# An MLP on one core: second product in one plain group and four groups of pairs, with half of its weights' sums made during the first product

## The chip, the core and the metric

The kernel runs on one core of a Trainium2 chip. The metric is the time of one execution on the device in microseconds (us); the median of three runs is compared.

The engines are named as the profile names them: PE multiplies matrices (PEld loads its weights), DVE, ACT and POOL work on vectors, and SP issues the transfers between the on-chip memory (SBUF, with PSUM for the products) and the DRAM. Each engine takes its instructions strictly in the order in which they stand in its queue. A matmul is given at 1.2 or 2.4 GHz; the profile's PEclk is the granted share of the higher one.

## What is computed

One layer of a decoder for 1032 columns of activations (1024 positions of a prompt and 8 sampled tokens), all in float32: an input projection, two groups of heads, an output projection, a norm, and the MLP that the change is about:

```python
x = layernorm(DN_ALPHA * x + mix, ln1_g, ln1_b)
h = jnp.square(jax.nn.relu(jnp.einsum('btd,df->btf', x, w_ff1)))   # 1024 -> 4096
x = layernorm(DN_ALPHA * x + jnp.einsum('btf,fd->btd', h, w_ff2), ln2_g, ln2_b)   # 4096 -> 1024
```

## The kernel before

Activations lie transposed: a tile is 128 features by 1032 columns, in two halves of 516 (`HN`), each in two pieces of 258 (`CH`). h has 32 such tiles. Every float32 operand X is split into hi (ACT rounds it, L111) and lo = X - hi (DVE or POOL, L112), and a product is hi.hi + hi.lo + lo.hi, so three matmuls; `split` and `product` (L1429 to L1440, matmul at L1438) are the helpers.

Most of the MLP runs by a scheme with seven products in place of eight (Strassen's, in Winograd's form). Weights are taken as 2x2 blocks A11, A12, A21, A22, the moving side as forms named B11, B21, B12, B22 and T1 to T4, where the T are sums of the B. The weights' sums are s1 = A21 + A22, s2 = s1 - A11, s4 = A12 - s2, s3 = A11 - A21. A unit makes its products in the order B21 (by A12), T1 (by s1), B11 (by A11), B22 (by s4), T2 (by s2), T3 (by s3), T4 (by A22).

**First product** (`ff1`, `pair`). The 32 tiles of h are made as 6 tiles without the scheme (`PLAIN`, in the stage before) and 13 pairs (`PAIRS`). A pair runs seven products of 24 matmuls, stores its four results B as tiles of `hd` in the DRAM, and for the pairs that the second product takes as pairs also the sums T1 to T4 in `ht`. `pair` loads two weight tiles `wpair`, makes s1 and s4 on DVE and s2 and s3 on POOL (L1464), evacuates PSUM with ACT and DVE, and stores.

**Second product** (`ff2`). It goes through `GROUPS` = [2, -3, -3, 2, -3, -3, 4]: a positive number is a plain group of so many tiles of h, a negative one a group of three pairs. A plain group (`plain_units`) has 16 units, one bank of PSUM each, added to `acc` by DVE (L1631, L1633). A group of pairs (`pair_units`, `pair_unit`) has four units q = 0 to 3 of seven products of 18 matmuls; a unit loads four blocks of weights into `w2raw` (six buffers), makes s1, s3, s4 on DVE and s2 on POOL (L1649), splits seven weights into `whi`/`wlo` or `wxh`/`wxl`, and adds seven times to `acc` (L1666).

What a group reads is loaded ahead, during the group before: a plain tile through `hraw` (two buffers), each of the 21 forms of a group of pairs through `hst` (four buffers, one row block of `hd` or `ht`), then split on ACT (t<-hst) and on DVE or POOL into one of 30 slots, which are used in turn (`RING`). After a plain group all 21 slots of the next group are free before it begins (`once`); after a group of pairs nine are (the forms B21, T1, B11, "early"), and the twelve others ("late") take slots that the last unit of the running group has still to read.

Within these loops the order on PE in the first product is as written; in the second product, and on the other engines everywhere, a scheduler with a simulated timeline sets the order of the queues at build time. SP has one queue: loads and stores of every kind stand in it one behind the other, each waiting for its buffer.

Of the kernel before, what the change touches and what calls it, by code (L numbers as in the profile page):

```python
# [9 lines left out]
F32 = mybir.dt.float32  # L10
F32R = mybir.dt.float32r
AF = mybir.ActivationFunctionType
OP = mybir.AluOpType
# [6 lines left out]
LBLK = [(0, 256), (768, 264), (256, 256), (512, 256)]  # L20
PBLK = [(0, 384), (384, 384), (768, 264)]
HN, CH = 516, 258
GROUPS = [2, -3, -3, 2, -3, -3, 4]
FIRST = [sum(abs(x) * (1 if x > 0 else 2) for x in GROUPS[:g]) for g in range(len(GROUPS))]
RING = "XXLLLLLLQBQBQBQBQBQBQBQQCQCQQB"
PLAIN = (0, 1, 14, 15, 28, 29)
PAIRS = [p for p in range(16) if 2 * p not in PLAIN]
FORMS = {"B11": "QL", "B21": "QL", "B12": "XX", "B22": "CL", "T1": "BQ", "T2": "BQ", "T3": "BQ", "T4": "BQ"}
TO = 2
TP = ((1, 3), (0, 1, 3), (0,), (2,))  # L30
LA = (384,384,384,256)
HE = {"B21": 0, "T1": 0, "B11": 0, "B22": 1, "T2": 1, "T3": 0, "T4": 1}
WE = (1, 0, 1, 0, 0, 0, 1, 1, 0, 1, 0)
# [26 lines left out]
class Kernel:  # L60
# [1305 lines left out]
    def out2(self, mixo, acc):  # L1366
        nc = self.nc
        V, G = nc.vector, nc.gpsimd
        self.fm = {}
        self.hd = self.dp.tile([32, 128, NT], F32, name="hd", tag="hd")  # L1370
        self.ht = self.dp.tile([14, 4, 128, HN], F32, name="ht", tag="ht")
        ws = self.resident(self.a["wout"][0], [self.x1slot("wr", w) for w in "LLLLLLBB"], self.tp)

        def units(c0):
            for n_ in range(8):
                ps = self.mmps(CH)
                yield from self.dense_q(ws[n_], mixo, c0, CH, ps)
                V.tensor_tensor(acc[n_][:, c0:c0 + CH], acc[n_][:, c0:c0 + CH], ps, op=OP.add)
                yield 3 * CH / 2400.0

        def norm(c, half, fill):
            put = (self.form("B11", c) + self.form("B21", c)) if not half else (self.form("B12", c) + self.form("B22", c))
            for wait in self.layer_norm_x1(acc, HN * half + CH * c, CH, put, LW[2 * c + half]):
                self.ahead(fill, wait)

        order = [(0, 0), (0, 1), (1, 0), (1, 1)]
        us = [units(HN * half + CH * c) for c, half in order]
        self.ahead(us[0], 99)
        chain = lambda *gs: (x for g in gs for x in g)
        norm(0, 0, chain(us[1], us[2]))  # L1390
        self.ahead(us[1], 99)
        norm(0, 1, chain(us[2], us[3]))
        self.ahead(us[2], 99)
        if TO == 0:
            self.t_forms(acc, 0)
        first = self.plain(0)
        norm(1, 0, chain(us[3], first))
        self.ahead(us[3], 99)
        if TO == 1:
            self.t_forms(acc, 0)  # L1400
        norm(1, 1, first)
        if TO == 2:
            self.t_forms(acc, 0)
        self.t_forms(acc, 1)
        self.ahead(first, 999)
        self.ahead(self.plain(1), 999)
# [46 lines left out]
    def pair(self, p):  # L1453
# [82 lines left out]
            out(f + 1, 0, P, m4)  # L1536
        yield

    def ff1(self):
        self.ps_ctx.close()  # L1540
        self.ps_ctx = ExitStack()
        self.sb = self.ps_ctx.enter_context(
            self.tc.tile_pool(name="sb", bufs=4, space=PSUM, reuse_waits="tile"))
        prev = iter(())
        for p in PAIRS:
            cur = self.pair(p)
            for i in range(5):
                next(cur)
                if i < 2:
                    next(prev, None)  # L1550
            prev = cur
        for _ in prev:
            pass
# [12 lines left out]
    def plain_forms(self, g, out):  # L1566
        nc = self.nc
        for j in range(GROUPS[g]):
            raw = self.h_load(FIRST[g] + j)
# [5 lines left out]
    def pair_forms(self, g, out):  # L1575
        n = -GROUPS[g]
        slots = {}
        once = GROUPS[g - 1] > 0
        early, late = ("B21", "T1", "B11"), ("B22", "T2", "T3", "T4")
# [39 lines left out]
    def plain_units(self, g, hs, acc):  # L1619
        V = self.nc.vector  # L1620
        nth = sum(1 for x in GROUPS[:g] if x > 0)
        for n_ in range(8):
# [13 lines left out]
    def pair_unit(self, g, q, fs, acc):  # L1636
        nc = self.nc
        V, G = nc.vector, nc.gpsimd
        E = lambda i: (V, G)[i]
        n = -128 * GROUPS[g]  # L1640
        A = {}
        for j in (1, 2, 3, 0):
            A[j] = self.tp.tile([128, 384], F32, name="w2raw", tag="w2raw", bufs=WB)[:, :n]
            nc.sync.dma_start(A[j], self.a["wff2_%d" % g][q][:, n * j:n * j + n])
        A11, A12, A21, A22 = (A[j] for j in range(4))

        def add(x, y, op, eng):
            z = self.wp.tile([128, 512], F32, name="wraw", tag="wraw", bufs=2)[:, :n]
            eng.tensor_tensor(z, x, y, op=op)  # L1649
            return z  # L1650
# [18 lines left out]
        product(Q, "B21", A12, E(WE[0]), True, True)  # L1669
        out(0, 0, Q)  # L1670
        yield
        s1 = add(A21, A22, OP.add, E(WE[1]))
        s2 = add(s1, A11, OP.subtract, E(WE[2]))
        T = self.bank()
        product(T, "T1", s1, E(WE[3]), True)
        out(1, 1, T)
# [2 lines left out]
        product(P, "B11", A11, E(WE[4]), True)  # L1679
        out(0, 0, P)  # L1680
        yield
        s4 = add(A12, s2, OP.subtract, E(WE[5]))
        product(T, "B22", s4, E(WE[6]), False, True)
        out(0, 1, T)
        yield
        product(P, "T2", s2, E(WE[7]), False)
        out(0, 1, P)
        yield
        s3 = add(A11, A21, OP.subtract, E(WE[8]))
        product(P, "T3", s3, E(WE[9]), False)  # L1690
        out(1, 1, P)
        yield
# [214 lines left out]
```

## Time and profile before

| | us |
|---|---|
| median of 3 runs | 1271.51 (1268.38 to 1274.57) |
| the profiled execution | 1271.54 |
| its span, first to last instruction | 1269.8 |
| PE busy in the span | 1210.6 (95%) |
| DVE, ACT, POOL busy | 833.7, 639.5, 509.0 |
| mean granted TensorE clock | 0.976 |

The profile is of one execution. Idle time of PE is what its row leaves open; a stretch at a granted clock of 1.00 without idle time runs at PE's pace. The first product lies at 629 to about 891 us from the span's start, the second from there to about 1208.

### The profile page before, as it was taken

The numbers are of one execution on the slowest core, as the hardware profiler recorded it, in microseconds if no ns is written. First come the engines' busy times: TensorE is split into PE (matmuls) and PEld (weight loads), VectorE is DVE, ScalarE is ACT, GpSimd is POOL, SyncE is SP. The second block draws the span as 40 slices with busy tenths as digits, with TensorE's granted clock in tenths as the row PEclk, the third lists the DMA queues.
The fourth block names the chain that finished last, engine by engine and source line by source line (L and its number), as shares of the span: only waits on it lengthen the run. The fifth ranks groups of instructions, "written<-read, shape, count | busy, mean of one in ns | idle before, by whom it ended". The sixth has DMA issues, their size and how long they took to land.

```text
span 1269.8 us, 25173 instructions
## 1 busy us (share of the span) xinstructions
PE 1210.6 (95%) x9268; PEld 1182.5 (93%) x9268; DVE 833.7 (66%) x1733; ACT 639.5 (50%) x1458; POOL 509.0 (40%) x540
## 2 busy tenths in 40 slices
PE   8999999889899899989999999999999999999996
PEld 7999999889899889989999999999989998989996
DVE  6477787778735885787743444444877768576667
ACT  5377676663656641267655555555545344242201
POOL 6243332362124651454533233332447542364214
PEclk9999999999989899899999999999989999989998
DMA  7322222132611261014435443444864535252202
GB/s 210 117 80 75 71 70 84 36 75 89 202 43 43 81 225 54 1 56 125 146 126 176 142 175 142 168 159 152 258 186 121 155 124 162 71 154 76 66 34 101
DMA packets 110075, 147.02 MB, mean 116 GB/s; under 512 B 30312, under 2 KB 65528, under 8 KB 109952
## 3 DMA queue, kind: packets, MB, share of 16 engines
q1 hardware_dynamic: 109952, 145.41, 36.6%
q8 instruction: 73, 1.20, 0.4%
q14 instruction: 50, 0.41, 0.1%
HBM read 100.31 MB, written 43.88 MB: 114 GB/s over the span
## 4 chain that ended last, share of the span: by engine, by line
PE 74%; DVE 12%; DMA 5%; issue 3%; ACT 3%; POOL 1%; SPq 1%; POOLq 0%; DVEq 0%; ACTq 0%
PE sb L1438 36%; PE mm L154 8%; PE mm L156 7%; PE mm L155 7%; DMA hst<-ht 2%; PE mm L1712 1%; PE mm L1714 1%; DVE wlo L112 1%; PE mm L1713 1%; DVE xB L1146 1%; DMA hst<-hd 1%; DVE acc L1132 1%; DMA hraw<-hd 1%; DVE uq L369 1%; DVE cx L303 1%
## 5 line engine op out<-in xcount | busy, mean ns | idle before, releaser
L112 POOL TENSOR_TENSOR wlo<-wraw,whi 128x512 fp32r<-128x512 f32 (+1 forms) x103 | 128.2, 1246 | 204.4 <-ACT whi L111 166.5
L111 ACT ACTIVATE whi<-wraw 128x512 fp32r<-128x512 f32 (+2 forms) x194 | 113.2, 585 | 169.8 <-PE sb L1438 105.9
L1438 PE MATMUL sb<-t,whi 128*128 128x258 f32 x1008 | 165.4, 287 | 6.4 <-ACT whi L111 4.8
L1438 PEld LDWEIGHTS sb<-t,whi 128*128 128x128 f32 x1008 | 141.4, 193 | 7.8 <-ACT whi L111 5.4
L1438 PE MATMUL sb<-xT,whi 128*128 128x258 f32 x832 | 133.8, 282 | 0.0
L154 PE MATMUL mm<-xhi,whi 128*128 128x344 f32 x384 | 126.3, 329 | 1.2 <-ACT zt L314 0.6
L155 PE MATMUL mm<-xlo,whi 128*128 128x344 f32 x384 | 123.9, 323 | 0.0
L156 PE MATMUL mm<-xhi,wlo 128*128 128x344 f32 x384 | 123.9, 323 | 0.0
L1438 PEld LDWEIGHTS sb<-xT,whi 128*128 128x128 f32 x832 | 114.0, 189 | 0.0
L1666 DVE TENSOR_TENSOR acc<-acc,sb 128x516 f32<-128x516 f32 x112 | 76.1, 686 | 56.5 <-PE sb L1438 56.4
L1438 PE MATMUL sb<-t,wlo 128*128 128x258 f32 x504 | 101.6, 286 | 3.0 <-DVE wlo L112 3.0
L1438 PE MATMUL sb<-xB,whi 128*128 128x258 f32 x624 | 100.2, 282 | 0.0
L112 DVE TENSOR_TENSOR wlo<-wraw,whi 128x512 fp32r<-128x512 f32 (+2 forms) x91 | 67.3, 743 | 42.5 <-ACT whi L111 42.5
L1438 PEld LDWEIGHTS sb<-xB,whi 128*128 128x128 f32 x624 | 85.7, 189 | 0.0
L1438 PE MATMUL sb<-xT,wlo 128*128 128x258 f32 x416 | 83.5, 282 | 0.0
L1438 PEld LDWEIGHTS sb<-t,wlo 128*128 128x128 f32 x504 | 79.0, 193 | 3.4 <-DVE wlo L112 3.4
L111 ACT ACTIVATE t<-hst 128x516 fp32r<-128x516 f32 x84 | 52.8, 634 | 51.0 <-DMA hst<-ht 23.9
L154 PEld LDWEIGHTS mm<-xhi,whi 128*128 128x128 f32 x384 | 72.4, 189 | 2.5 <-ACT sraw L295 1.1
L155 PEld LDWEIGHTS mm<-xlo,whi 128*128 128x128 f32 x384 | 72.4, 189 | 0.4 <-issue 0.4
L156 PEld LDWEIGHTS mm<-xhi,wlo 128*128 128x128 f32 x384 | 72.4, 188 | 0.4 <-issue 0.4
L112 POOL TENSOR_TENSOR t<-hst,t 128x516 fp32r<-128x516 f32 x36 | 52.3, 1459 | 35.4 <-ACT t L111 35.3
L1481 DVE TENSOR_TENSOR hst<-sb,hst 128x516 f32<-128x516 f32 x40 | 27.7, 694 | 58.9 <-PE sb L1438 58.9
(512 smaller groups left out, 3527.3 us busy)
## 6 DMA issues: line engine op xcount, KB each, us to landing
hd<-hst SPq DMA_DIRECT2D x52, 258.0 KB
wpair<-in_wff SPq DMA_DIRECT2D x26, 512.0 KB
ht<-hsum SPq DMA_DIRECT2D x48, 258.0 KB
hst<-ht SPq DMA_DIRECT2D x48, 258.0 KB
w2raw<-in_wff SPq DMA_DIRECT2D x64, 192.0 KB
wraw<-in_win SPq DMA_DIRECT2D x40, 256.0 KB
hst<-hd SPq DMA_DIRECT2D x36, 258.0 KB
wraw<-in_wff SPq DMA_DIRECT2D x24, 256.0 KB
```

The lines of the kernel that those rows point to most:

```text
L111: nc.scalar.activation(hi, src, AF.Copy)
L112: (lo_eng or nc.vector).tensor_tensor(lo, src, hi.bitcast(F32), op=OP.subtract)
L154: nc.tensor.matmul(ps, hi[:, k % 4, :], mh, start=(k == 0), stop=False)
L155: nc.tensor.matmul(ps, hi[:, k % 4, :], ml, start=False, stop=False)
L156: nc.tensor.matmul(ps, lo[:, k % 4, :], mh, start=False, stop=(k == last))
L303: nc.vector.scalar_tensor_tensor(out, raw[:, j:j + NP], cw[:, t, j:j + 1], out, op0=OP.mult, op1=OP.add)
L369: V.scalar_tensor_tensor(u[:, cc], ps[cc // 2][:, cc % 2], self.s2[:, hc:hc + 1], dt[:, cc, None, :].to_broadcast([128, 2, 128]), op0=OP.m ...
L1132: V.scalar_tensor_tensor(x, x, self.lnp[:, 0, i:i + 1], rb, op0=OP.mult, op1=OP.mult)
L1146: nc.vector.scalar_tensor_tensor(lo, x, b, hi.bitcast(F32), op0=OP.add, op1=OP.subtract)
L1438: self.nc.tensor.matmul(ps[:, 512 * c:512 * c + CH], a[:, k, :], forms[c][k][b], start=(start and k == 0 and a is hi and b == 0), stop=(st ...
L1481: V.tensor_tensor(h3, self.banks(ps), h3, op=OP.add)
L1666: V.tensor_tensor(a, a, self.banks(ps), op=OP.add)
```

## The change

`GROUPS` becomes [4, -3, -3, -3, -3, 4], and `PLAIN` the tiles 0 to 3, 28 and 29. So the two plain groups of two tiles become one of four at the start, and the four groups of pairs follow one another. The number of matmuls stays.

For seven of the 16 units of pairs (`STORED`: q = 0 and q = 3 of groups 1, 2, 3, and q = 0 of group 4) the four sums of weights are made earlier. After the pairs 0, 1, 2, 4, 6, 8, 10 of the first product (`BATCH`) `weight_load` loads the four blocks of one unit into two slots (`wq`) that are idle in that stage, and `weight_sums` makes the sums in place on DVE within the next pair and stores them in the DRAM (`wd`). `keep_in_program_order` ties these loads and sums to their written place. In the second product such a unit loads seven tiles (A12, s1, A11, s4, s2, s3, A22) into the same six `w2raw` buffers, where it loaded four and made the sums.

```diff
-GROUPS = [2, -3, -3, 2, -3, -3, 4]
+GROUPS = [4, -3, -3, -3, -3, 4]
-PLAIN = (0, 1, 14, 15, 28, 29)
+PLAIN = (0, 1, 2, 3, 28, 29)
+BATCH = (0, 1, 2, 4, 6, 8, 10)
+STORED = [(g, q) for g in range(1, 5) for q in (0, 3) if (g, q) != (4, 3)]
...
+    def weight_load(self, i):
+        g, q = STORED[i]
+        n = -128 * GROUPS[g]
+        z = []
+        for j in range(2):
+            t = self.x1slot("wq", "X").bitcast(F32)
+            self.tc.keep_in_program_order(
+                self.nc.sync.dma_start(t[:, :2 * n], self.a["wff2_%d" % g][q][:, 2 * n * j:2 * n * j + 2 * n]))
+            z += [t[:, 0:n], t[:, n:2 * n]]
+        return i, n, z
+
+    def weight_sums(self, i, n, z):
+        A11, A12, A21, A22 = z
+        for k, o, x, y, op in ((0, A22, A21, A22, OP.add), (2, A21, A11, A21, OP.subtract),
+                               (1, A11, A22, A11, OP.subtract), (3, A12, A12, A11, OP.subtract)):
+            self.tc.keep_in_program_order(self.nc.vector.tensor_tensor(o, x, y, op=op))
+            self.nc.sync.dma_start(self.wd[i, k][:, :n], o)
...
         prev = iter(())
-        for p in PAIRS:
+        batch = None
+        for n_, p in enumerate(PAIRS):
             cur = self.pair(p)
             for i in range(5):
                 next(cur)
                 if i < 2:
                     next(prev, None)
+                if i == 1 and batch:
+                    self.weight_sums(*batch)
+            batch = self.weight_load(BATCH.index(n_)) if n_ in BATCH else None
             prev = cur
...
-        for j in (1, 2, 3, 0):
+        stored = STORED.index((g, q)) if (g, q) in STORED else None
+        for j in (1, 4, 0, 7, 5, 6, 3) if stored is not None else (1, 2, 3, 0):
             A[j] = self.tp.tile([128, 384], F32, name="w2raw", tag="w2raw", bufs=WB)[:, :n]
-            nc.sync.dma_start(A[j], self.a["wff2_%d" % g][q][:, n * j:n * j + n])
...
+            nc.sync.dma_start(A[j], self.a["wff2_%d" % g][q][:, n * j:n * j + n] if j < 4 else
+                              self.wd[stored, j - 4][:, :n])
...
+        def add(k, x, y, op, eng):
+            if stored is not None:
+                return A[3 + k]
```

Three places show how the queues move. DVE, in the first product, where one pair follows the other. Before:

```order
L1489 TENSOR_TENSOR hsum<-hst,hsum 128x516
L1464 TENSOR_TENSOR wraw<-wpair 128x512
L1481 TENSOR_TENSOR hst<-sb,hst 128x516
L112 TENSOR_TENSOR wlo<-wpair,whi 128x512
L112 TENSOR_TENSOR wlo<-wraw,whi 128x512
L1481 TENSOR_TENSOR hst<-sb,hst 128x516
```

After:

```order
L1492 TENSOR_TENSOR hsum<-hst,hsum 128x516
L1557 TENSOR_TENSOR wq<-wq 128x384
L1467 TENSOR_TENSOR wraw<-wpair 128x512
L1484 TENSOR_TENSOR hst<-sb,hst 128x516
L1557 TENSOR_TENSOR wq<-wq 128x384
L114 TENSOR_TENSOR wlo<-wpair,whi 128x512
L1557 TENSOR_TENSOR wq<-wq 128x384 x2
L114 TENSOR_TENSOR wlo<-wraw,whi 128x512
```

Of the four new sums two stand ahead of the low part of the pair's first weight, and two ahead of that of its second.

SP, at the end of the first product (in_wff_0 holds the weights of the first plain group, in_wff_1 and wd those of the first group of pairs). Before:

```order
L1558 DMA hraw<-hd 128x1032
L1484 DMA hd<-hst 128x516
L1558 DMA hraw<-hd 128x1032
L1644 DMA w2raw<-in_wff_1 128x384 x2
L1609 DMA wraw<-in_wff_0 128x256
L1644 DMA w2raw<-in_wff_1 128x384 x4
```

After:

```order
L1487 DMA hd<-hst 128x516
L1583 DMA hraw<-hd 128x1032 x2
L1670 DMA w2raw<-in_wff_1 128x384
L1634 DMA wraw<-in_wff_0 128x512
L1670 DMA w2raw<-wd 128x384
L1670 DMA w2raw<-in_wff_1 128x384
L1670 DMA w2raw<-wd 128x384 x3
L1634 DMA wraw<-in_wff_0 128x512
L1614 DMA hst<-hd 128x516
L1583 DMA hraw<-hd 128x1032
L1487 DMA hd<-hst 128x516
```

The first tile of h now stands behind a store, and the third, which the plain group of four also needs at its start, behind the weights.

ACT, where one group of pairs follows another: w2raw_12479 and wraw_12542 are the first and second weight of unit q = 0 of the new group (for B21 and T1), the t are its late forms. Before, from group 1 to group 2:

```order
L111 ACTIVATE t_12233<-hst_12231 128x516
L111 ACTIVATE whi_12488<-w2raw_12479 128x384
L111 ACTIVATE t_12263<-hst_12261 128x516
L111 ACTIVATE t_12291<-hst_12289 128x516
L111 ACTIVATE whi_12547<-wraw_12542 128x384
L111 ACTIVATE h_12538<-hraw_12536 128x1032
```

After, from group 2 to group 3 (w2raw_13587 and w2raw_13589 are those two weights, the second of them a stored s1; wxh_13625 is a weight of the unit before):

```order
L113 ACTIVATE t_13307<-hst_13305 128x516
L113 ACTIVATE wxh_13625<-w2raw_13412 128x384
L113 ACTIVATE t_13336<-hst_13334 128x516
L113 ACTIVATE whi_13602<-w2raw_13587 128x384
L113 ACTIVATE t_13341<-hst_13339 128x516
L113 ACTIVATE t_13371<-hst_13369 128x516
L113 ACTIVATE whi_13659<-w2raw_13589 128x384
```

The weight for T1 comes from a load in place of a sum, and stands behind the same two forms as before.

## Rows read from the trace of the kernel before

**Rows 1.** The page: the chain that ended last, by engine.

```profile
PE 74%; DVE 12%; DMA 5%; issue 3%; ACT 3%; POOL 1%; SPq 1%; POOLq 0%; DVEq 0%; ACTq 0%
```

**Rows 2.** By stretch: length; PE, PEld, DVE, ACT, POOL busy (count); PEclk, DMA share, GB/s.

```profile
629.00:888.00 259.00, 259.00 (x2159) 259.00 (x2158) 110.27 (x164) 139.92 (x233) 84.43 (x65) 1.00 0.44 154
888.00:912.00 24.00, 24.00 (x202) 24.00 (x201) 18.33 (x29) 13.59 (x25) 8.74 (x6) 1.00 0.86 276
912.00:933.00 21.00, 17.25 (x114) 16.41 (x114) 17.20 (x24) 11.58 (x21) 15.65 (x12) 0.84 0.72 209
...
977.00:995.00 18.00, 15.21 (x122) 14.60 (x122) 16.14 (x17) 9.95 (x18) 16.94 (x12) 1.00 0.63 196
...
1046.00:1075.00 29.00, 26.74 (x213) 25.71 (x213) 23.74 (x39) 12.89 (x27) 8.30 (x7) 1.00 0.54 161
...
1129.00:1143.00 14.00, 11.03 (x68) 10.60 (x67) 9.95 (x11) 6.58 (x11) 8.47 (x7) 0.76 0.57 172
1143.00:1160.00 17.00, 15.63 (x126) 15.10 (x125) 12.49 (x15) 5.28 (x11) 9.29 (x7) 1.00 0.32 94
...
1202.00:1209.00 7.00, 5.43 (x44) 5.01 (x43) 1.67 (x3) 0.00 (x0) 0.00 (x0) 1.00 0.00 0
```

**Rows 3.** PE's queue in order of time: start, length, [idle before, releaser].

```profile
925.40 1.23 PE L1438 MATMUL sb<-t,whi 128*128 128x258 f32 x4 [2.80 <-ACT whi L111]
...
979.85 0.39 PE L1438 MATMUL sb<-t,whi 128*128 128x258 f32 x1 [0.93 <-ACT whi L111]
981.73 0.51 PE L1438 MATMUL sb<-t,wlo 128*128 128x258 f32 x2 [1.14 <-DVE wlo L112]
990.91 0.76 PE L1438 MATMUL sb<-t,whi 128*128 128x258 f32 x4 [0.72 <-DVE acc L1666]
```

**Rows 4.** ACT's queue ahead of the wait at 979.85.

```profile
976.50 0.64 ACT L111 ACTIVATE t<-hst 128x516 fp32r<-128x516 f32 x1 [1.61 <-DMA hst<-hd]
977.05 0.51 ACT L111 ACTIVATE whi<-w2raw 128x384 fp32r<-128x384 f32 x1
978.04 1.34 ACT L111 ACTIVATE t<-hst 128x516 fp32r<-128x516 f32 x2 [0.48 <-DMA hst<-ht]
979.29 0.51 ACT L111 ACTIVATE whi<-wraw 128x384 fp32r<-128x384 f32 x1
```

**Rows 5.** SP's queue: the loads of those forms.

```profile
974.80 1.48 SPq L1589 DMA_DIRECT2D hst<-ht  x3
```

**Rows 6.** DVE and POOL at the same place.

```profile
980.03 1.65 DVE L112 TENSOR_TENSOR wlo<-wraw,whi 128x384 fp32r<-128x384 f32 x1
...
985.74 0.55 DVE L1649 TENSOR_TENSOR wraw<-w2raw,wraw 128x384 f32<-128x384 f32 x1
...
979.45 1.81 POOL L112 TENSOR_TENSOR t<-hst,t 128x516 fp32r<-128x516 f32 x1
```

**Rows 7.** Form splits on ACT (tile t) while the first plain group runs.

```profile
895.00:926.00 31.00, 7.49 (x57) 7.20 (x58) 10.37 (x12) 12.71 (x20) 11.46 (x8) 0.98 0.81 243
```

**Rows 8.** Groups of instructions, 888 to 1209: the sums of weights, and the adds.

```profile
L1649 DVE TENSOR_TENSOR wraw<-w2raw 128x384 f32<-128x384 f32 x32 | 32.7, 1040 | 2.5 <-POOL wlo L112 1.5 <-POOL wxl L112 0.8
L1649 POOL TENSOR_TENSOR wraw<-wraw,w2raw 128x384 f32<-128x384 f32 x16 | 18.1, 1132 | 18.3 <-DVE wlo L112 11.7 <-PE sb L1438 4.3 <-DMA w2raw<-in_wff 1.8
L1633 DVE TENSOR_TENSOR acc<-acc,sb 128x516 f32<-128x516 f32 x16 | 10.6, 684 | 1.2 <-PE sb L1438 1.2
```

**Rows 9.** First product: DVE ahead of a pair's first weight, and PE's use of it.

```profile
719.28 0.68 DVE L112 TENSOR_TENSOR wlo<-wpair,whi 128x512 fp32r<-128x512 f32 x1
...
721.36 0.64 PE L1438 MATMUL sb<-xT,whi 128*128 128x258 f32 x4
721.84 0.40 PE L1438 MATMUL sb<-xT,wlo 128*128 128x258 f32 x2
```

**Rows 10.** Tiles of h at the end of the first product: SP's load, ACT's split.

```profile
882.49 0.42 SPq L1558 DMA_DIRECT2D hraw<-hd  x1
...
888.32 1.07 ACT L111 ACTIVATE h<-hraw 128x1032 fp32r<-128x1032 f32 x1 [0.34 <-DMA hraw<-hd]
```

More of the change, by code (lines that the diff above doesn't have):

```diff
@@ L1370, in out2 @@
         self.hd = self.dp.tile([32, 128, NT], F32, name="hd", tag="hd")
+        self.wd = self.dp.tile([len(STORED), 4, 128, 384], F32, name="wd", tag="wd")
         self.ht = self.dp.tile([14, 4, 128, HN], F32, name="ht", tag="ht")
@@ L1641, in pair_unit @@
         A = {}
-        for j in (1, 2, 3, 0):
+        stored = STORED.index((g, q)) if (g, q) in STORED else None
+        for j in (1, 4, 0, 7, 5, 6, 3) if stored is not None else (1, 2, 3, 0):
             A[j] = self.tp.tile([128, 384], F32, name="w2raw", tag="w2raw", bufs=WB)[:, :n]
-            nc.sync.dma_start(A[j], self.a["wff2_%d" % g][q][:, n * j:n * j + n])
-        A11, A12, A21, A22 = (A[j] for j in range(4))
-        def add(x, y, op, eng):
+            nc.sync.dma_start(A[j], self.a["wff2_%d" % g][q][:, n * j:n * j + n] if j < 4 else
+                              self.wd[stored, j - 4][:, :n])
+        A11, A12, A21, A22 = (A.get(j) for j in range(4))
+        def add(k, x, y, op, eng):
+            if stored is not None:
+                return A[3 + k]
             z = self.wp.tile([128, 512], F32, name="wraw", tag="wraw", bufs=2)[:, :n]
@@ L1671, in pair_unit @@
         yield
-        s1 = add(A21, A22, OP.add, E(WE[1]))
-        s2 = add(s1, A11, OP.subtract, E(WE[2]))
+        s1 = add(1, A21, A22, OP.add, E(WE[1]))
+        s2 = add(2, s1, A11, OP.subtract, E(WE[2]))
         T = self.bank()
@@ L1681, in pair_unit @@
         yield
-        s4 = add(A12, s2, OP.subtract, E(WE[5]))
+        s4 = add(4, A12, s2, OP.subtract, E(WE[5]))
         product(T, "B22", s4, E(WE[6]), False, True)
@@ L1688, in pair_unit @@
         yield
-        s3 = add(A11, A21, OP.subtract, E(WE[8]))
+        s3 = add(3, A11, A21, OP.subtract, E(WE[8]))
         product(P, "T3", s3, E(WE[9]), False)
```

## Prediction

> **What bounds the kernel now.** I read the chain that ended last first: PE holds 74% of it [rows 1], so time is gained only where PE stops or runs at its lower clock. The table by stretch says where in the MLP that is [rows 2]. In the first product PE is busy for 259.00 of 259.00 us at a clock of 1.00: nothing is to be gained there, and the change can only cost. The second product loses time in patches. Idle time is length less PE's busy time: 3.75 us at 912 to 933, where the first plain group hands over to the first group of pairs; 2.79 at 977 to 995, between two groups of pairs; 2.26 at 1046 to 1075, around the second plain group; 2.97 and 1.37 at 1129 to 1160, again between two groups of pairs; 1.57 at 1202 to 1209, at the end. That is 14.7 us. Twice PE stops long enough for the clock to fall to the lower of its two levels for a while: 21 us at 0.84 and 14 us at 0.76 are 3.4 us each. So 21.5 us are lost in all; the four stretches of the second product that are not shown run full. If the change took all of it, the profiled execution of 1271.5 us (its span is 1269.8; the median of the runs, 1271.51, is the same number) would take 1250: the floor.
>
> Then I read what ends the waits. At 925.40 and 979.85 it is ACT's high part of a weight, at 981.73 DVE's low part, at 990.91 DVE's add to acc [rows 3]. ACT was not busy before 979.85: its queue holds two forms ahead of that weight, which waited for their loads [rows 4], and those loads were issued one by one, as buffers of hst came free [rows 5]. The low part then took 1.65 us on DVE, where a sum of the same size takes 0.55, while POOL ran a form's low part from 979.45 to 981.26 [rows 6]. So a switch between groups of pairs is a queue of late forms through four buffers, in which a weight that PE needs stands behind.
>
> **The start of the second product (cost).** The plain group of four needs four tiles of h, of which hraw holds two. A tile's load took from 882.49 to 888.32, 5.8 us [rows 10]. In the new order of SP the first two leave together after a store, at about 882.5, and land by 889; their splits end near 890.3 and 892.6, and PE, which ends the first product at about 891.4, starts with them on four banks. The third tile's load can leave when the first's low part is done, 890.3, and lands at 896; PE has used up the first two tiles after 48 matmuls, at 0.12 us each (four start in 0.48 us) [rows 9], 5.8 us, at 897.2. Third and fourth tile then come within a microsecond of need. I put 1.0 us here, between 0 and 3.
>
> **From the plain group to the first group of pairs (gain).** Before, 21 forms have the time of 16 units of 12 matmuls, 23 us; ACT made 20 form splits in 31 us [rows 7], so the forms are late, and the stretch loses 3.75 + 3.4 = 7.2 us [rows 2]. Now the units have 24 matmuls, 46 us, in which that pace gives 30. I leave 0.3 us, between 0 and 3.75. Of DVE's adds to acc 16 of 0.68 us go as well [rows 8], 11 us of an engine that is idle for more; alone they are worth nothing, as are the eight weight splits that become wider. The second plain group's 2.26 us go with that group, but in its place stands a switch between two groups of pairs.
>
> **The three switches between groups of pairs.** There were two, at 2.79 and, with its clock and the stretch behind it, 2.97 + 3.4 + 1.37 = 7.7 us [rows 2]. Removed near each are the sums of two units (one unit at the last): per unit three on DVE, 2 x 1.04 + 0.56 = 2.6 us, and one on POOL, 1.13 us [rows 8], that also blocked POOL's queue while it waited for DVE. Seven units: 18 us of DVE and 8 of POOL, nearly all beside PE's work, so their sum is no gain; what counts is the order on ACT. There the weight for T1 stands behind the same two late forms as before; it no longer waits for a sum, but it was not the sum that held it. For group 1 to 2 slots and order are as before; DVE's add that ended late at 990.91 stood behind work that goes. I take 2.0, between 0 and 7.7.
>
> The switches from 2 to 3 and 3 to 4 are new in kind: the late forms take slots in another order, and three of them can be split only when the old group's last unit has done its third product (B11), where before six had gone by then. From there I count on ACT: two waiting forms 1.28, the low part that frees a buffer 0.70, the next load about 2.7 (the third load of rows 5 was issued at about 976.0, and its split, the second of the two at 978.04, began at 978.7 [rows 4]), then four forms at 0.64 and three weights at 0.51 [rows 4], the last of them T1's: 8.8 us. PE has 58 matmuls in that time, T4 of the unit before, B22, T2 and four of the new B21: 7.0 us. It is 1.8 us late, and the low parts behind it on DVE and POOL add some 1.2, as at 981.73 [rows 3]: 3.0 us each. Nothing in the trace shows such a switch; if the reading fails it costs nothing, or, with the form queue late as at the first group as well, 7.2 more. I take 3.0, nearest to the 2.79 of rows 2.
>
> **The sums in the first product (cost).** 28 sums of 0.55 us alone [rows 6], 2.2 us in seven pairs of 20 us, of which DVE is busy 43% [rows 2]. Two stand ahead of the low part of a pair's first weight. That low part ended at 719.96, PE used it at 721.84 [rows 9]: 1.1 us fit into 1.9. The 14 loads and 28 stores, 11 MB more at 154 GB/s, stand on SP among stores that nobody waits for and ahead of weight loads for which wpair has the buffers of two pairs. I put 0 here. The cover is that 1.9 us.
>
> **The sum.** 1.0 + 0.3 + 2.0 + 3.0 + 3.0 + 1.6 at the end (unchanged, and not shortened: that unit is not stored) = 10.9 us lost, where 21.5 were. 1271.5 - 10.6 = **1261 us**.
>
> **The rivals.**
> *The first product pays.* DVE took 1.65 us for what takes 0.55 alone, with POOL at work [rows 6]. Were both sums ahead of the low part held up by a POOL instruction of 1.3 us, they would take 3.7 us, 1.8 more than the margin, in seven pairs: 12.6 us, **1273.5**. Against it: POOL is busy for a third of that stretch [rows 2]. The Trainium skill, SBUF — State Buffer, section "Who interferes with whom", says that a DVE instruction with two inputs in SBUF contends with a GpSimd instruction that reads SBUF, and that the one that starts later is blocked for the whole of the other; by that rule each of the 28 new sums could wait so, and rows 6 agree.
> *The clock falls at both new switches.* 3.4 us each [rows 2] on top of 3.0: **1268**. [...]
> *The sums were not it, and switches stay as they were*, three at the mean of 2.8 and 7.7: 15.8 + 2.9 lost, **1269**.
> *Switches without waits*, since ACT, DVE and POOL run ahead once the sums are gone: at most 1 us each, **1256**, in good runs 1253.
> *Slower: the forms starve.* A stored unit issues seven weight loads in place of four, on the queue in which the forms' loads stand, and into six buffers, so SP waits in front of a weight while a form's buffer is free. If at every switch the forms come as late as they did at the first group, 7.2 us with the clock on top of 3.0, the three cost 30.6 and the whole 33.5: 1271.5 + 12.0 = **1283.5**. It decides from 8.3 us per switch (25 for the three, to lose 27.9). For it: forms already came by load, not by slot [rows 4]. Against: the DMA share there is 0.32 to 0.63, and was 0.86 and 0.72 where the forms were late [rows 2].
>
> **How the numbers follow.** Forecast, 1256 to 1266: 0.50. No waits at the switches: 0.12. Clock at the new switches: 0.15. Sums were not it: 0.05. First product pays: 0.08. Forms starve: 0.10. A measurement of this kernel tells some 0.5% from no change, 1265.2 to 1277.9. Faster than that: 0.12 and all but the upper edge of the forecast, 0.60. Slower: 0.10. Within: 0.30. For 8 times in 10 the range runs from 1253 to 1275; it leaves out the starving forms and the ends of the others.
>
> **What would show it.** In the profile after: the first product at 1.00 and without idle time (if not, the first product pays); a full stretch where plain tiles give way to the first pairs, and no low clock there; three switches some 60 us apart, each with a wait for ACT's high part of T1's weight behind forms, longer at the second and third. Wrong would be the prediction if ACT's waits for forms at the switches were gone, or if PE waited there for forms (t) themselves and not for weights.

## The result, and the profile after

The changed kernel takes 1263.73 us (median of six runs, 1262.25 to 1266.08) where the kernel before took 1271.25 beside it: a ratio of 0.9943, interval 0.9925 to 0.9961. The forecast was 1261 and faster, range 1253 to 1275. The profiled execution took 1262.84 us, its span is 1260.7.

First the stretches of the changed kernel that the argument needs, with the columns of [rows 2]: length; PE, PEld, DVE, ACT, POOL busy (count); PEclk, DMA share, GB/s.

```profile
629.00:888.00 259.00, 259.00 (x2159) 259.00 (x2158) 123.14 (x192) 138.29 (x232) 84.33 (x65) 1.00 0.57 196
...
893.00:908.00 15.00, 13.50 (x108) 12.87 (x107) 8.43 (x11) 9.01 (x15) 5.11 (x3) 1.00 0.99 335
908.00:990.00 82.00, 82.00 (x685) 82.00 (x684) 52.79 (x77) 32.98 (x60) 33.53 (x27) 1.00 0.50 151
990.00:1012.00 22.00, 19.81 (x161) 19.20 (x160) 13.17 (x20) 12.00 (x23) 14.45 (x12) 1.00 0.82 258
...
1060.00:1090.00 30.00, 26.75 (x215) 25.88 (x214) 21.73 (x32) 12.85 (x26) 13.60 (x12) 1.00 0.68 206
...
1120.00:1128.00 8.00, 7.41 (x61) 7.20 (x61) 4.79 (x6) 5.53 (x10) 8.00 (x7) 1.00 0.69 213
...
1140.00:1150.00 10.00, 7.75 (x65) 7.54 (x64) 9.11 (x12) 3.42 (x6) 6.41 (x4) 1.00 0.38 112
...
1188.00:1200.00 12.00, 11.21 (x93) 11.00 (x92) 3.66 (x6) 0.00 (x0) 0.16 (x1) 1.00 0.14 45
```

The clock is 1.00 in every stretch; both falls of [rows 2] are gone in this execution. (Its mean clock over the whole span is 0.982; the five other executions list 0.976 to 0.979. So the clock was lower somewhere in them; where, no profile shows.) Length less PE's busy time is 1.50 us at the start, 0 from the plain group into the first pairs, 2.19, 3.25 and 0.59 + 2.25 at the three switches between groups of pairs, 0.79 at the end; with 0.08 at 1128 to 1140, not shown, 10.65 us in all. Before it was 14.7 us, and 6.8 more were lost by the low clock.

Then PE's waits of more than 0.25 us in the second product, in order of time, as in [rows 3]:

```profile
899.74 1.78 PE L1441 MATMUL sb<-h,whi 128*128 128x258 f32 x10 [0.59 <-ACT h L113]
905.04 0.51 PE L1441 MATMUL sb<-h,whi 128*128 128x258 f32 x2 [0.88 <-POOL h L114]
1000.55 0.75 PE L1441 MATMUL sb<-t,whi 128*128 128x258 f32 x4 [1.98 <-ACT whi L113]
1063.29 0.75 PE L1441 MATMUL sb<-t,whi 128*128 128x258 f32 x4 [1.12 <-ACT whi L113]
1073.28 0.75 PE L1441 MATMUL sb<-t,whi 128*128 128x258 f32 x4 [1.43 <-DVE acc L1695]
1083.23 0.51 PE L1441 MATMUL sb<-t,wxl 128*128 128x258 f32 x2 [0.54 <-DVE wxl L114]
1127.79 0.75 PE L1441 MATMUL sb<-t,whi 128*128 128x258 f32 x4 [0.59 <-ACT whi L113]
1147.95 0.51 PE L1441 MATMUL sb<-t,wxl 128*128 128x258 f32 x2 [2.25 <-DVE wxl L114]
1196.90 0.75 PE L1441 MATMUL sb<-t,wxh 128*128 128x258 f32 x4 [0.79 <-DVE acc L1695]
```

Each of the three switches begins with a wait for ACT's high part of a weight (1.98, 1.12, 0.59). The waits at 1073, 1083 and 1147 are for DVE, and no step of the prediction put them there.

The first switch is the one foretold. ACT, POOL and SP there:

```profile
997.33 0.63 ACT L113 ACTIVATE t<-hst 128x516 fp32r<-128x516 f32 x1 [1.78 <-DMA hst<-ht]
999.45 0.63 ACT L113 ACTIVATE t<-hst 128x516 fp32r<-128x516 f32 x1 [1.48 <-DMA hst<-ht]
999.99 0.51 ACT L113 ACTIVATE whi<-w2raw 128x384 fp32r<-128x384 f32 x1
...
992.62 3.04 POOL L114 TENSOR_TENSOR t<-hst,t 128x516 fp32r<-128x516 f32 x2 [0.33 <-ACT t L113]
...
994.50 0.32 SPq L1614 DMA_DIRECT2D hst<-ht  x1
994.88 0.43 SPq L1670 DMA_DIRECT2D w2raw<-wd  x1
995.41 0.85 SPq L1614 DMA_DIRECT2D hst<-ht  x2
```

The weight for T1 stands on ACT behind a form, split at 999.45, that waited for its load. That load is the first of the two at 995.41. Its buffer had come free at 993.93, with the first of POOL's two low parts; but on SP it stood behind the load of 994.50, which waited for a buffer until DVE's low part ended at 994.48, and behind a weight's. From its issue to the form's split it took 4.0 us, where the load of 994.50 took 2.8 to the split at 997.33.

The last big wait has another origin. DVE and POOL ahead of 1147.95:

```profile
1142.63 2.93 DVE L114 TENSOR_TENSOR wr<-hst,wr 128x512 fp32r<-128x512 f32 x1
1145.48 1.35 DVE L114 TENSOR_TENSOR wlo<-w2raw,whi 128x384 fp32r<-128x384 f32 x1
1146.75 0.68 DVE L1695 TENSOR_TENSOR acc<-acc,sb 128x516 f32<-128x516 f32 x1
1147.35 0.55 DVE L114 TENSOR_TENSOR wxl<-wraw,wxh 128x384 fp32r<-128x384 f32 x1
...
1142.26 2.75 POOL L114 TENSOR_TENSOR h<-hraw,h 128x1032 fp32r<-128x1032 f32 x1
1144.95 1.46 POOL L1678 TENSOR_TENSOR wraw<-wraw,w2raw 128x384 f32<-128x384 f32 x1
```

The preparation of the last plain group is at work here: the low part of one of its weights (wr) takes 2.93 us on DVE, where the six of its kind that ran beside no POOL instruction took 0.68 to 0.69, and it ends 0.55 us after POOL is done with a tile of h. The next low part takes 1.35 for 0.55, beside POOL's sum. The low part that PE needs (wxl) stands behind both and behind an add.

### The profile page after: what moved, and what is told of

The parts are those of the page before. It is cut to its first block, busy times and chain, and to the rows that moved or that the text cites. A ratio compares the mean times of both kernels' runs of the same rounds, so it can differ in the third digit from the quotient of the medians.

```text
span 1260.7 us, 25210 instructions
## 1 busy us (share of the span) xinstructions
PE 1205.4 (96%) x9268; PEld 1177.4 (93%) x9268; DVE 811.1 (64%) x1716; ACT 637.3 (51%) x1450; POOL 497.4 (39%) x533
## 4 chain that ended last, share of the span: by engine, by line
PE 74%; DVE 13%; DMA 5%; ACT 3%; issue 3%; POOL 2%; SPq 0%; POOLq 0%; DVEq 0%; ACTq 0%
PE sb L1441 37%; PE mm L156 7%; PE mm L158 7%; PE mm L157 7%; DMA hst<-ht 1%; PE mm L1741 1%; DMA xraw<-in_xT 1%; DVE xB L1148 1%; DMA hst<-hd 1%; PE mm L1742 1%; PE mm L1743 1%; DVE acc L1134 1%; DVE wlo L114 1%; DMA hraw<-hd 1%; DVE cx L305 1%
## 5 line engine op out<-in xcount | busy, mean ns | idle before, releaser
L114 POOL TENSOR_TENSOR wlo<-wraw,whi 128x512 fp32r<-128x512 f32 (+1 forms) x88 | 109.1, 1241 | 188.6 <-ACT whi L113 167.9
L113 ACT ACTIVATE whi<-wraw 128x512 fp32r<-128x512 f32 (+1 forms) x164 | 100.3, 611 | 146.6 <-PE sb L1441 83.6
L1441 PE MATMUL sb<-t,whi 128*128 128x258 f32 x1008 | 162.5, 284 | 5.5 <-ACT whi L113 3.7
L1441 PEld LDWEIGHTS sb<-t,whi 128*128 128x128 f32 x1008 | 138.6, 190 | 6.7 <-ACT whi L113 4.3
L114 DVE TENSOR_TENSOR wlo<-wraw,whi 128x512 fp32r<-128x512 f32 (+1 forms) x76 | 57.1, 752 | 27.4 <-ACT whi L113 26.9
```

What stands on the lines that cost most here:

```text
L113: nc.scalar.activation(hi, src, AF.Copy)
L114: (lo_eng or nc.vector).tensor_tensor(lo, src, hi.bitcast(F32), op=OP.subtract)
L1441: self.nc.tensor.matmul(ps[:, 512 * c:512 * c + CH], a[:, k, :], forms[c][k][b], start=(start and k == 0 and a is hi and b == 0), stop=(st ...
```

## The experiments

The second column is the median with its ratio to the kernel before, the third PE's idle time from 893 to 1200 us of the profiled execution, the fourth the granted clock there. Waits at the very end of the second product lie behind 1200 us in the slower executions: 1.57 us for the kernel before, 0.78 each for the new grouping alone and the stored sums alone. "Unread" sums are made and stored in the first product but not used in the second.

| kernel | us, ratio (interval) | idle | PEclk |
|---|---|---|---|
| before | 1271.25 | 13.13 | 0.98 |
| after | 1263.73, 0.9943 (0.9925 to 0.9961) | 10.65 | 1.00 |
| new grouping alone | 1265.49, 0.9959 (0.9944 to 0.9974) | 11.07 | 0.98 |
| stored sums alone | 1267.09, 0.9966 (0.9951 to 0.998) | 10.99 | 0.99 |
| new grouping, stored sums unread | 1268.70, 0.9979 (0.9965 to 0.9993) | 11.68 | 0.99 |
| after + six form buffers | 1263.03, 0.9936 (0.992 to 0.9951) | 8.97 | 0.99 |
| after + tiles of h on DVE | 1259.72, 0.9919 (0.9888 to 0.9951) | 6.51 | 0.99 |
| after + forms on DVE | 1255.79, 0.9878 (0.9859 to 0.9898) | 4.65 | 1.00 |
| after + all three | 1248.63, 0.9824 (0.9801 to 0.9846) | 2.19 | 1.00 |
| new grouping + all three | 1253.79, 0.9864 (0.9833 to 0.9895) | 4.06 | 1.00 |
| the same, stored sums unread | 1252.52, 0.985 (0.9833 to 0.9867) | 4.05 | 1.00 |
| before + all three | 1256.16, 0.9889 (0.9864 to 0.9914) | 5.56 | 0.99 |
| after + all three, POOL without work | 1247.48, 0.9805 (0.9783 to 0.9828) | 0.90 | 1.00 |

Each ratio is taken beside its own runs of the kernel before. Where two intervals overlap, the medians alone do not tell the two kernels apart: so it is, among others, for the changed kernel against either half of the change, six form buffers or tiles of h on DVE, and for all three edits against POOL without work.

### The change in two halves

**New grouping alone.**

```diff
-BATCH = (0, 1, 2, 4, 6, 8, 10)
-STORED = [(g, q) for g in range(1, 5) for q in (0, 3) if (g, q) != (4, 3)]
+BATCH = ()
+STORED = []
...
-        self.wd = self.dp.tile([len(STORED), 4, 128, 384], F32, name="wd", tag="wd")
```

> The changed kernel with the new grouping alone: STORED and BATCH are empty, so all 16 units of pairs make their four sums in place and the first product makes none. My theory (grouping brings the first half, the stored sums shorten the switches): the handover from plain tiles to the first pairs stays full, as after the change, and the start of the second product loses about 1.5 us, but the three switches between groups of pairs lose what the two of before lost, 2.8 to 7.7 us each, about 15 in all in place of 8.4; some 1269 us. Rival 'the grouping is all of it': the same as the changed kernel, 1263 to 1265 us, with about 8 us at the switches. Rival 'without the stored sums the new order does not pay': 1272 us or more, with a low clock at two switches.

It took 1265.49 us where I had put 1269, next to the rival that the grouping is all of it (1263 to 1265): it brings more of the gain than I had given it, and what the sums add to it, 1.8 us, is not clear of the noise. Start and first handover lose about 1 us together. The three largest of PE's waits:

```profile
1079.89 0.72 PE L1440 MATMUL sb<-t,whi 128*128 128x258 f32 x4 [2.20 <-DVE acc L1694]
1132.65 0.51 PE L1440 MATMUL sb<-t,wlo 128*128 128x258 f32 x2 [2.37 <-POOL wlo L114]
1152.33 0.74 PE L1440 MATMUL sb<-t,wxl 128*128 128x258 f32 x2 [2.40 <-DVE wxl L114]
```

They are waits for low parts and adds, not for ACT's weights, and in this execution (1268.5 us, the longest of the six) the clock falls at every switch: 0.94 in 985 to 1015, 0.95 in 1055 to 1090, 0.96 in 1115 to 1160, some 5.3 us. The five shorter runs list a mean clock of 0.978 to 0.982 over the whole execution, this one 0.974: the profile shows a run that lost more to the clock than the median did.

**Stored sums alone.**

```diff
-GROUPS = [4, -3, -3, -3, -3, 4]
+GROUPS = [2, -3, -3, 2, -3, -3, 4]
...
-PLAIN = (0, 1, 2, 3, 28, 29)
+PLAIN = (0, 1, 14, 15, 28, 29)
...
-STORED = [(g, q) for g in range(1, 5) for q in (0, 3) if (g, q) != (4, 3)]
+STORED = [(g, q) for g in (1, 2, 4, 5) for q in (0, 3) if (g, q) != (5, 3)]
```

> The old grouping (2, three pairs, three pairs, 2, three pairs, three pairs, 4) with seven units whose sums are made in the first product: q = 0 and 3 of the first three groups of pairs, q = 0 of the last. My theory: the loss from the first plain group to the first pairs (7.2 us with the low clock) and the 2.3 us around the second plain group stay, and the two switches between groups of pairs fall from 10.5 us to about 4; some 1265 us. Rival 'the grouping is all of it': 1270 to 1272 us, as before. Rival 'the stored sums do all of it': 1263 us.

It took 1267.09 us, 2 above my figure. The two switches and the second plain group:

```profile
980.21 0.75 PE L1441 MATMUL sb<-t,whi 128*128 128x258 f32 x4 [2.40 <-ACT whi L113]
1057.16 0.75 PE L1441 MATMUL sb<-h,whi 128*128 128x258 f32 x4 [1.60 <-DVE acc L1695]
1061.10 0.75 PE L1441 MATMUL sb<-h,whi 128*128 128x258 f32 x4 [0.78 <-DVE acc L1658]
1130.51 0.74 PE L1441 MATMUL sb<-t,whi 128*128 128x258 f32 x4 [2.06 <-ACT whi L113]
```

The second plain group loses 2.4 us, where I had left 2.3. The two switches wait 4.5 us where I had put about 4 with the clock in it, and at the second the clock fell all the same (0.96 in 1115 to 1160, 1.8 us more). The handover to the first pairs, which I had left at 7.2, lost 3.2 us here without a low clock. Alone, the grouping gave 0.41% and the sums 0.34%; together 0.57%, less than the two added, though the intervals do not exclude that they add up.

### What the sums cost in the first product

```diff
-        stored = STORED.index((g, q)) if (g, q) in STORED else None
+        stored = None
```

> As the first of these kernels (new grouping, all sums in place in the second product), but the first product still loads, makes and stores the 28 sums of seven units, which nobody reads. So it measures what the sums cost in the first product. My theory: nothing there; the first product takes 262 us as before and after, and the time is that of the first kernel within 1 us. Rival 'the first product pays': DVE's two sums ahead of a pair's low part hold up PE for up to 1.8 us in each of seven pairs, 1 to 12 us above the first kernel.

> The kernel with the unread sums a second time, for another profile. Its median was 1268.7 us, 3.2 above that of the grouping alone, with runs from 1263.5 to 1272.4, though its first profile showed the first product at 262.16 us as in the changed kernel. If the unread sums cost time in some executions, a profile of a run above 1268 shows it in the first product (over 263 us) or in waits there; my theory is that the first product takes 262.2 us again and the difference lies in clock and waits of the second product or ahead of the MLP.

> New grouping, six form buffers, all forms and plain tiles on DVE, sums in place in the second product, and in the first product the 28 sums that nobody reads. Against the kernel without those sums (1253.8 us) it measures once more what they cost in the first product, on a second product with few waits. My theory: nothing, 1252.5 to 1255 us, the first product at 262.2 us. Rival 'they cost time in some executions' (the earlier pair of kernels differed by 3.2 us in the median): 1256 to 1258 us, with a wider spread of the runs.

The first pair did not settle it: 1268.70 us against 1265.49, with runs from 1263.5 to 1272.4. The two profiles (1266.05 and 1264.67 us) show the first product at 262.16 us, as without the sums, but neither is of a run above 1268, so what made the long ones long stays open. The second pair, on a second product with few waits, shows no cost: 1252.52 with the unread sums, 1253.79 without, and 262.16 us for the first product in both; the intervals leave room for some 3 us. In the changed kernel the tile of the sums has these rows (duration ns least, median, most; first and last start):

```profile
L1557 DVE TENSOR_TENSOR wq<-wq x28: 543/548/559, 659.4 to 864.4; 128x384 f32<-128x384 f32 x28
L1558 SPq DMA_DIRECT2D wd<-wq x28: 319/382/1646, 660.0 to 865.1; - x28
```

All 28 sums take the 0.55 us of [rows 6], none is held up. Nor could POOL hold one up: in this execution none of the 28 ran beside a POOL instruction.

### Four buffers or POOL

**Six buffers for forms.** Every third form of a switch goes through hraw, which is free then.

```diff
-        slots = {}
+        slots, used = {}, []
...
-            raw = self.hst()
+            if once or len(used) % 3:
+                raw = self.hst()
+            else:
+                raw = self.tp.tile([128, NT], F32, name="hraw", tag="hraw", bufs=2)[:, :HN]
+            used.append(t)
```

> The changed kernel, with six buffers for the forms at the three switches between groups of pairs in place of four: every third form of such a group is loaded through the two buffers of hraw, which hold no tile of h then. My theory (the weight for T1 stands on ACT behind forms whose loads wait for one of four buffers): the waits for ACT's high part at the three switches, 1.98, 1.12 and 0.59 us, and the one of 1.43 for an add to acc behind late forms fall to under 1.5 us together, and the time falls by 3 to 4 us to about 1260. Rival 'the forms wait for slots that the old group's last unit still reads, not for buffers': the waits stay within 1 us of 5.1 in all, 1263 to 1264. Rival 'DMA time is the limit there' (share 0.82 and 0.83 at two of the switches): loads that leave earlier land no earlier, and the time stays or grows by 1 us.

The waits for ACT's weights went, the one for an add (1.43 us) that I had named with them did not, and the time stayed (1263.03 us). PE's waits at the switches now:

```profile
997.47 0.50 PE L1441 MATMUL sb<-t,wlo 128*128 128x258 f32 x2 [0.27 <-DVE wlo L114]
1062.19 0.76 PE L1441 MATMUL sb<-t,wxh 128*128 128x258 f32 x4 [0.63 <-DVE acc L1699]
1069.06 0.75 PE L1441 MATMUL sb<-t,whi 128*128 128x258 f32 x4 [2.00 <-DVE acc L1699]
1123.51 0.75 PE L1441 MATMUL sb<-t,whi 128*128 128x258 f32 x4 [0.23 <-ACT whi L113]
1126.04 0.51 PE L1441 MATMUL sb<-t,wlo 128*128 128x258 f32 x2 [1.79 <-DVE wlo L114]
```

Waits for ACT fell from 3.69 to 0.23 us; waits for DVE's low parts and adds have come up in their place, 4.7 us where 1.97 were (1.43 and 0.54), and the clock falls in two stretches (0.95 in 1055 to 1090, 0.96 in 1115 to 1160), 3.5 us that the changed kernel's profile did not lose. The buffers were the first limit, DVE's queue the one right behind it.

**Tiles of h on DVE.**

```diff
-            self.split(raw, hi, lo, lo_eng=(nc.vector, nc.gpsimd)[j % 2])
+            self.split(raw, hi, lo, lo_eng=nc.vector)
```

> The changed kernel, with the low part of every plain tile of h made on DVE; two of a group's four were made on POOL. It tests two waits: 0.88 us for POOL's h at the start of the second product, and 2.25 us for DVE's wxl at 1147.95, where DVE's low part of a weight of the last plain group took 2.93 us (0.68 alone) while POOL made a tile's low part from 1142.26 to 1145.01. My theory (DVE was blocked by POOL): the 2.25 us go, or shrink below 0.7, and the start loses 0.5 to 1.5 us; 1260 to 1262 us. Rival 'DVE has too much queued there': the wait stays at 1.5 us or more, since DVE now makes the tile's low part as well, some 1.1 us each; 1263 to 1265.

1259.72 us, with two runs at 1257 and two at 1262 to 1263; the profile is of the shortest. In it the 2.25 us at 1147.95 and both waits at the start are gone (0.04 us idle from 893 to 908), although DVE makes the tiles' low parts as well: its busy time from 893 to 1200 us is 193.17 us, where it was 193.13.

**Forms on DVE.**

```diff
-HE = {"B21": 0, "T1": 0, "B11": 0, "B22": 1, "T2": 1, "T3": 0, "T4": 1}
+HE = {"B21": 0, "T1": 0, "B11": 0, "B22": 0, "T2": 0, "T3": 0, "T4": 0}
```

> The changed kernel, with the low parts of all forms made on DVE; those of B22, T2 and T4 were made on POOL, 1.3 us each alone and 1.3 to 1.8 beside DVE, where DVE takes 0.7. My theory says that the switches wait for form buffers and for low parts held up by POOL: buffers then come free sooner, and DVE's low parts take 0.55 to 0.7 more often; the waits at the three switches, 8.3 us, fall to 4 to 6, 1260 to 1262 us. Rival 'DVE is then the late engine': nine forms per group at 0.7 are 6.3 us more on DVE at each switch, the adds to acc come late, and the waits stay or grow; 1263 to 1268.

1255.79 us, better than I had put it: at the switches no wait for a weight of ACT is left and no wait of more than 0.6 us. This edit alone does more than six buffers. Two reasons are at hand, and the run doesn't separate them: a low part on DVE gives its buffer back after 0.7 us where POOL took 1.44 on average, and DVE has less of POOL beside it (89.76 us from 893 to 1200, where it was 139.41).

**All three.**

> The changed kernel with six form buffers, all forms' low parts and all plain tiles' low parts on DVE: the three together. With six buffers alone the waits for ACT's weights had gone (3.69 to 0.23 us), and waits for low parts and adds on DVE had come up beside it (0.27, 2.63, 1.79, 2.26 us). If those come from DVE being blocked by POOL, as I think, they fall to under 2.5 us in all and no stretch has a low clock: 1257 to 1260 us. Rival 'DVE is then the late engine': 1262 us or more, with waits for DVE's adds.

1248.63 us, below the range I gave. PE idles for 2.19 us in 307.

**POOL without work in the groups of pairs.** All three, and WE, the table of the engines for the pair units' low parts and sums, set to DVE throughout.

```diff
-WE = (1, 0, 1, 0, 0, 0, 1, 1, 0, 1, 0)
+WE = (0, 0, 0, 0, 0, 0, 0, 0, 0, 0, 0)
```

> The kernel of 1248.6 us (stored sums, six form buffers, forms and tiles on DVE), and now also the low parts of all weights of the pair units and the sums of the nine units that make them in place on DVE: POOL does nothing in the groups of pairs. If what is left of the waits still came from POOL (low parts of weights of 1.0 us on POOL, DVE blocked beside them), the 2.0 us of waits fall below 1: 1246 to 1249 us. Rival 'DVE is the late engine': POOL had 80 us of work there of which DVE takes about 45, which brings DVE from 212 to some 255 us in the 307 from 893 on; adds and low parts come late at the switches, 1252 us or more.

1247.48 us: level with the 1248.63 of the three edits, and not slower. DVE is not the late engine: PE's only wait of more than 0.25 us is the 0.78 at the end. DVE is now busy for 230.67 of the 307 us, POOL for 0.00, PE for 306.10; of the changed kernel these were 193.13, 139.41 and 296.35. Groups of instructions on DVE in the second product (count | busy, mean ns of one): first the changed kernel's forms, weights and adds, then those of this one, whose other 21 forms come through hraw:

```profile
L114 DVE TENSOR_TENSOR t<-hst,t 128x516 fp32r<-128x516 f32 x48 | 42.7, 900 | 27.9 <-ACT t L113 27.7
L114 DVE TENSOR_TENSOR wxl<-w2raw,wxh 128x384 fp32r<-128x384 f32 x9 | 7.2, 796 | 0.0
L1695 DVE TENSOR_TENSOR acc<-acc,sb 128x516 f32<-128x516 f32 x108 | 73.8, 687 | 59.7 <-PE sb L1441 59.1
...
L114 DVE TENSOR_TENSOR t<-hst,t 128x516 fp32r<-128x516 f32 x63 | 42.8, 691 | 6.7 <-ACT t L113 6.6
L114 DVE TENSOR_TENSOR wxl<-w2raw,wxh 128x384 fp32r<-128x384 f32 x19 | 10.5, 551 | 0.0
L1699 DVE TENSOR_TENSOR acc<-acc,sb 128x516 f32<-128x516 f32 x112 | 77.3, 690 | 47.8 <-PE sb L1441 47.3
```

Without POOL beside it DVE makes 63 forms in the time of 48. The adds to acc, with one operand in PSUM, take 0.69 us either way.

### The same three edits without the change, and with half of it

> The new grouping with all sums made in place in the second product (none in the first), and the three edits that took the changed kernel to 1248.6 us: six form buffers, all low parts of forms and of plain tiles on DVE. It asks whether the sums made in the first product are still worth anything once DVE is not blocked by POOL. If the stored sums helped because they took work from DVE and POOL where these block each other (my theory), little is left of their gain: 1249 to 1252 us, with sums in place on DVE at 0.55 to 1.0. Rival 'the switches need the sums out of the way, whatever POOL does' (DVE then makes forms, sums and adds): 1254 us or more, with waits for sums or adds at the three switches.

> The kernel before with the same three edits and nothing of the change. It asks whether the loss from the first plain group to the first pairs (3.75 us idle and 3.4 us of low clock) was one of time (21 forms in 16 units of 12 matmuls, as my prediction says) or of DVE and POOL blocking each other. My theory: the switches between groups of pairs shrink from 10.5 us to under 2, the loss at the first handover stays at 4 to 7 us and so do about 2 us around the second plain group; 1257 to 1262 us. Rival 'contention was all of it': the handover falls below 2 us too, 1249 to 1254 us. Rival 'DVE has no room for forms in the short plain groups': the handover grows, 1264 us or more.

The kernel before with the three edits takes 1256.16 us, with the new grouping too 1253.79, with the stored sums too 1248.63. So the change is still worth 7.5 us, 2.4 by the grouping and 5.2 by the sums (3.9 against the kernel with unread sums). Taken in this order, the grouping brought 0.41% and the sums 0.16% on the kernel as it was, 0.25% and 0.40% here; the intervals are nearly as wide as these steps, so that the shares turned round is likely and not shown. That the sums would be worth little there was wrong: with the new grouping and the three edits, every run that uses them is shorter than every run that does not. At the first handover the kernel before with the edits still loses time:

```profile
908.00:930.00 22.00, 19.27 (x152) 18.40 (x152) 22.00 (x34) 13.80 (x26) 8.98 (x7) 1.00 0.68 203
930.00:985.00 55.00, 54.20 (x432) 53.28 (x432) 46.40 (x68) 24.43 (x45) 22.49 (x18) 0.97 0.53 161
```

2.73 us of waits and about 1.7 us of clock, of 7.2: DVE is busy without a break there. So more than half of that loss stays with POOL busy for 8.98 of 22 us, where it was 15.65 of 21 [rows 2], which fits the lack of time that the prediction named; but the edits gave DVE those forms to make, so that this run alone doesn't separate the two. The waits around the second plain group went entirely, which I had not expected.

## Why the prediction held, step by step

**Start of the second product: 1.0 forecast, 1.50 measured.** The third tile was late by 0.59 us and the fourth by 0.88: each within a microsecond of need, as foretold, but the 1.0 stood for both. The fourth tile's low part takes 2.40 us on POOL; with the tiles' low parts on DVE both waits were gone.

**Plain group to first pairs: 0.3 forecast, 0 measured.** The clock held as well. It is the grouping that did it: alone it lost 0.44 us there, the stored sums alone 3.2.

**Switches: 2.0, 3.0, 3.0 forecast; 2.19, 3.25, 2.92 measured.** The sums are right and the reasons only partly. For group 1 to 2 the reading held: T1's weight stood behind a late form. For the other two the step that failed is the count on ACT from B11 on, which made T1's weight 1.8 us late, later than at the first switch: it was less late, 1.12 and 0.59 us against 1.98. One of its terms was too small at that: the load of the form ahead, put at 2.7 us, took 3.8 and 3.6 from its issue to the split there (1058.40 to 1062.19, 1123.12 to 1126.69), and 4.0 at the first switch. What filled the terms up was of another kind: 4.2 us (1.43, 0.54 and 2.25) are waits that the prediction had not placed. That the three terms come to 8.4 where 8.0 were forecast is luck in that part. At 1073.28 DVE's add stood behind low parts of late forms:

```profile
1070.75 0.69 DVE L114 TENSOR_TENSOR t<-hst,t 128x516 fp32r<-128x516 f32 x1 [0.91 <-ACT t L113]
1071.93 0.70 DVE L114 TENSOR_TENSOR t<-hst,t 128x516 fp32r<-128x516 f32 x1 [0.49 <-ACT t L113]
1072.54 0.68 DVE L1695 TENSOR_TENSOR acc<-acc,sb 128x516 f32<-128x516 f32 x1
```

At 1147.95 it was POOL's tile of h against DVE's weight, nothing of the switch at all; with the tiles on DVE that wait was gone. Of the signs that I named, "longer at the second and third" is therefore refuted.

**The end: 1.6 forecast, 0.79 measured.** Before, PE waited twice for DVE's add, 0.78 us each; now once. With the new grouping alone it also waits once, with the stored sums alone twice. Why is not shown.

**The sums in the first product: 0 forecast, 0 measured.** 262.52 us from the first matmul of the pairs to the last before, 262.16 after.

**The sum.** 10.65 us lost where 10.9 were forecast: that it comes so close owes something to errors that cancel, 0.5 too little at the start, 0.3 and 0.8 too much at the handover and the end. The profiled execution is nevertheless 1.8 us above the 1261: its first product begins at 630.93, before it was 629.10. That start moves between 626.8 and 631.8 in the profiles of these kernels, whose code ahead of it differs only in which tiles of h are made there.

**The rivals.** "The first product pays" falls: the 28 rows take 0.55 us, PE has no idle time in the first product, and the second pair of kernels shows no cost. Its reason was not put to the test there, since no POOL instruction ran beside any of the 28. In the second product such a loss shows: 2.93 us for 0.68, and 900 ns for 691 in the mean of the forms, for instructions with both inputs in SBUF, and no change for those that read PSUM. The Trainium skill, SBUF — State Buffer, section "Who interferes with whom", was cited there as its reason: a DVE instruction with two inputs in SBUF contends with a GpSimd instruction that reads SBUF. By that section the one that starts later is blocked. The trace agrees: the row of 2.93 us began 0.37 us after POOL's and ended 0.55 us after it.

"The clock falls at both new switches" did not come in the profiled execution (1.00 in 1060 to 1150). "Switches without waits" is refuted by 8.4 us of them. "The sums were not it" is half true: without them the grouping gives 5.4 of the 7.5 us, but not by switches left as they were, and the rest is not clear of the noise. "Forms starve" falls: it needed 8.3 us at each switch, and the worst lost 3.25.

**What is not settled.** Whether the edits to the low parts gain by freeing DVE from being blocked, or by POOL's own 1.4 us for what DVE does in 0.69, was not taken apart: each edit does both. The changed kernel's trace has a case of each. DVE ahead of the second switch, POOL ahead of the third, each with the load that took the buffer:

```profile
1055.25 3.12 DVE L114 TENSOR_TENSOR t<-hst,t 128x516 fp32r<-128x516 f32 x2 [1.50 <-ACT t L113]
1058.40 0.80 SPq L1614 DMA_DIRECT2D hst<-ht  x2
...
1121.35 3.01 POOL L114 TENSOR_TENSOR t<-hst,t 128x516 fp32r<-128x516 f32 x2
1123.12 1.58 SPq L1614 DMA_DIRECT2D hst<-ht  x2
```

The first load at 1058.40 brought the form that stood ahead of T1's weight, and left when DVE's second low part was done, 1.79 us long for 0.69; the first at 1123.12 did so at the third switch, and left when POOL's first was done, 1.75 us long.

## What to carry to other kernels

When forms, weights and adds go through one chain of buffers, ask of each engine how long it holds a buffer, not only how busy it is: POOL had room, and moving its low parts of forms and tiles to the busier DVE gave, with two more buffers, twice what the change gave. A wait removed at the head of a queue pays only when the next one in line is not just behind it; here six buffers paid nothing alone. And judge two halves of a change on a kernel without the shared bottleneck too: the sums, whose share could not be told from noise on the kernel as it was, showed a clear one there.

## What the runs showed of the hardware

DVE is slowed beside POOL where both its inputs lie in SBUF, and not where one lies in PSUM. In the second product of the changed kernel (893 to 1200 us) 74 adds to acc ran beside a POOL instruction, 38 beside none, and all took 0.68 to 0.70 us. Of the 48 low parts of forms (0.69 us alone) 21 ran beside no POOL instruction, and 8 began before the one that ran beside them: all 29 took 0.68 to 0.70 us. The other 19 began while a POOL instruction ran; they took 0.73 to 1.79 us, and each of them ended 0.55 to 0.56 us after that instruction did. So in this trace DVE waits for the end of the POOL instruction that began first, and a low part that begins first isn't slowed.

And waits of the same size came with a low clock in one execution and not in another: the changed kernel kept 1.00 through waits of 1.98 and 2.25 us, the kernel with six buffers shows 0.95 in the 35 us around a wait of 2.00, so that part of them ran at 1.2 GHz in place of 2.4. What tells the two cases apart is not shown.
